# Gate and up products of 12 of 22 feature tiles as seven half products over a 2x2 block split

## The chip, the cores and the metric

The kernel runs on one core of a Trainium2 chip. The metric is device time in microseconds (us); the time before is 1137.3 us, the median of three runs (1135.86, 1137.30 and 1139.14). The engines are named as in the profile: PE is the matrix engine (PEld its loads of weights), DVE is VectorE, ACT is ScalarE, POOL is GpSimd, and SP issues the DMAs.

## The reference, cut to what matters

One layer for 512 tokens of width 1024: a SwiGLU half, a mixing stage (attention and a recurrence), and a second SwiGLU half. The change lies in the two SwiGLU halves alone:

```
def swiglu(x, w_gate, w_up, w_down):           # w_gate, w_up: 1024 x 2816; w_down: 2816 x 1024
    return (jax.nn.silu(x @ w_gate) * (x @ w_up)) @ w_down

x = x + 0.5 * swiglu(rms_norm(x, norm_ffn1), ffn1_gate, ffn1_up, ffn1_down)
...                                             # mixing
x = x + 0.5 * swiglu(rms_norm(x, norm_ffn2), ffn2_gate, ffn2_up, ffn2_down)
```

## The kernel before

The activations lie transposed: eight tiles `X[k]` of 128 features x 512 tokens. Every fp32 product is done as three matmuls of the reduced type fp32r, in `mm3` (L176 to L179): each operand is split into a high part, its cast to fp32r, and a low part, the remainder. The three are high x high (L177), high weights x low activations (L178) and low weights x high activations (L179). For a block of weights `load_split` (L154 to L164) does a DMA of 128x512, a cast on ACT (L162) and a subtraction on DVE (L163).

In `ffn` a SwiGLU half has 22 feature tiles of 128 features. For one tile, `dense` makes the gate product, 8 blocks of depth (k) x 3 matmuls of 512 columns into one PSUM bank, then the up product in the same way: 48 matmuls from four loaded blocks. The RMS norm's gain is in the split activations `xs`; its scale per token, `S`, is multiplied to both results on DVE (L296, L300). ACT does the Silu, POOL the product `h`, and `split` makes `h` into high and low (L189, L190). When the 22 hidden tiles are there, eight down products of 22 blocks x 3 matmuls follow, and DVE adds half of each to `X[m]`.

The order of work is set by a scheduler that lists the instructions of each engine by priority, in the program's order unless an instruction is not ready; tiles lie in pools with a fixed number of buffers (`NB`, `NM`, and `NW` = 3 for a raw, high or low weight block), and an instruction that writes a buffer waits until its last reader is done. Every engine then runs its list strictly in order. All weight DMAs are issued by SP, in order too.

## Time and profile before

| | |
|---|---|
| median of three runs | 1137.3 us |
| profiled execution, own time | 1135.56 us |
| its span, first to last instruction | 1133.8 us |
| first SwiGLU half: gate and up, then down | to 249 us, to 369 us |
| mixing stage | 369 to 763 us |
| second half: gate and up, then down | to 1010 us, to 1130 us |
| matmuls in the program | 6499 |
| loads of weights, of X | 256 KB each |

A matmul's row in the trace shows a start and a modelled end: the rows of successive matmuls overlap, and what one costs in a stream is the distance between starts. Names in the rows drop buffer numbers, so `g` is any gate result and `u` any up result; `wh` and `wl` are the high and low parts of a weight block, `xh` and `xl` those of the activations.

### The profile page before, as it was taken

The numbers are of one execution on the slowest core, as the hardware profiler recorded it, in microseconds if no ns is written. First come the engines' busy times: TensorE is split into PE (matmuls) and PEld (weight loads), VectorE is DVE, ScalarE is ACT, GpSimd is POOL, SyncE is SP. The second block draws the span as 40 slices with busy tenths as digits, with TensorE's granted clock in tenths as the row PEclk, the third lists the DMA queues.
The fourth block names the chain that finished last, engine by engine and source line by source line (L and its number), as shares of the span: only waits on it lengthen the run. The fifth ranks groups of instructions, "written<-read, shape, count | busy, mean of one in ns | idle before, by whom it ended". The sixth has DMA issues, their size and how long they took to land.

```text
span 1133.8 us, 16807 instructions
## 1 busy us (share of the span) xinstructions
PE 1105.7 (98%) x6499; PEld 870.7 (77%) x6499; DVE 567.3 (50%) x966; ACT 445.6 (39%) x782; POOL 182.6 (16%) x135
## 2 busy tenths in 40 slices
PE   8999999999999998999999998999999999999998
PEld 6888888888888766866677665777888888888887
DVE  7444443443333466487777777674434444433322
ACT  6333333333323553364644654553333333322221
POOL 1111111120001233221311312041111111110000
PEclk9999999999999999999999999998999999999999
DMA  5332333233333224311302102022333232334442
GB/s 203 100 96 93 102 93 102 93 90 102 99 93 104 90 66 112 88 47 40 75 27 53 39 23 57 11 74 93 93 101 96 94 102 93 103 90 116 115 114 68
DMA packets 67231, 97.79 MB, mean 86 GB/s; under 512 B 19280, under 2 KB 21456, under 8 KB 67152
## 3 DMA queue, kind: packets, MB, share of 16 engines
q1 hardware_dynamic: 67152, 96.73, 29.0%
q8 instruction: 51, 0.84, 0.3%
q14 instruction: 28, 0.23, 0.1%
HBM read 93.03 MB, written 3.67 MB: 85 GB/s over the span
## 4 chain that ended last, share of the span: by engine, by line
PE 87%; DVE 8%; ACT 2%; issue 1%; DMA 1%; SPq 0%; DVEq 0%; ACTq 0%
PE g L179 7%; PE g L178 7%; PE g L177 7%; PE dn L178 7%; PE dn L177 7%; PE u L179 7%; PE dn L179 7%; PE u L177 7%; PE u L178 7%; PE inv L566 2%; PE z L691 2%; PE o L717 1%; PE k L177 1%; PE k L179 1%; PE k L178 1%
## 5 line engine op out<-in xcount | busy, mean ns | idle before, releaser
L162 ACT CAST wh<-w 128x512 fp32r<-128x512 f32 (+1 forms) x315 | 192.1, 610 | 412.9 <-PE dn L178 146.6
L163 DVE TENSOR_TENSOR wl<-w,wh 128x512 fp32r<-128x512 f32 (+1 forms) x294 | 200.2, 681 | 246.4 <-ACT wh L162 245.7
L179 PE MATMUL g<-xh,wl 128*128 128x512 f32 x352 | 138.1, 392 | 1.9 <-DVE wl L163 1.9
L177 PE MATMUL u<-xh,wh 128*128 128x512 f32 x352 | 137.2, 390 | 2.6 <-ACT wh L162 2.6
L178 PE MATMUL g<-xl,wh 128*128 128x512 f32 x352 | 138.1, 392 | 0.7 <-DVE xl L193 0.7
L177 PE MATMUL g<-xh,wh 128*128 128x512 f32 x352 | 138.2, 393 | 0.1
L179 PE MATMUL u<-xh,wl 128*128 128x512 f32 x352 | 137.1, 390 | 0.0
L178 PE MATMUL u<-xl,wh 128*128 128x512 f32 x352 | 137.1, 389 | 0.0
L302 POOL TENSOR_TENSOR h<-sg,u 128x512 f32<-128x512 f32 x44 | 69.1, 1571 | 395.8 <-DVE u L300 386.2
L177 PE MATMUL dn<-hdh,wh 128*128 128x512 f32 x240 | 93.4, 389 | 0.0
L178 PE MATMUL dn<-hdl,wh 128*128 128x512 f32 x240 | 93.4, 389 | 0.0
L179 PE MATMUL dn<-hdh,wl 128*128 128x512 f32 x240 | 93.4, 389 | 0.0
L179 PEld LDWEIGHTS g<-xh,wl 128*128 128x128 f32 x352 | 66.8, 190 | 16.2 <-DVE wl L163 2.3
L177 PEld LDWEIGHTS u<-xh,wh 128*128 128x128 f32 x352 | 66.1, 188 | 17.1 <-ACT wh L162 3.3
L178 PEld LDWEIGHTS g<-xl,wh 128*128 128x128 f32 x352 | 66.6, 189 | 15.0 <-DVE xl L193 1.1
L177 PEld LDWEIGHTS g<-xh,wh 128*128 128x128 f32 x352 | 66.7, 189 | 14.7 <-ACT sq L134 0.5
L178 PEld LDWEIGHTS u<-xl,wh 128*128 128x128 f32 x352 | 66.2, 188 | 13.7
L179 PEld LDWEIGHTS u<-xh,wl 128*128 128x128 f32 x352 | 66.1, 188 | 13.6
L300 DVE TENSOR_TENSOR u<-u,S 128x512 f32<-128x512 f32 x44 | 30.4, 691 | 65.7 <-PE u L179 65.7
L163 POOL TENSOR_TENSOR wl<-w,wh 128x512 fp32r<-128x512 f32 x22 | 30.4, 1384 | 137.6 <-ACT wh L162 102.6
L177 PEld LDWEIGHTS dn<-hdh,wh 128*128 128x128 f32 x240 | 45.1, 188 | 9.4
L179 PEld LDWEIGHTS dn<-hdh,wl 128*128 128x128 f32 x240 | 45.1, 188 | 9.3
(268 smaller groups left out, 1798.6 us busy)
## 6 DMA issues: line engine op xcount, KB each, us to landing
w<-wgu SPq DMA_DIRECT2D x176, 256.0 KB, 2.6
w<-wd SPq DMA_DIRECT2D x80, 256.0 KB, 2.6
w<-wrw SPq DMA_DIRECT2D x28, 256.0 KB, 2.6
w<-wqk SPq DMA_DIRECT2D x16, 256.0 KB, 2.6
wv<-wv SPq DMA_DIRECT2D x16, 256.0 KB, 2.6
wo<-wo SPq DMA_DIRECT2D x16, 256.0 KB, 2.6
x<-xT SPq DMA_DIRECT2D x8, 256.0 KB, 5.4
w<-wd SPq DMA_DIRECT2D x16, 128.0 KB, 2.0
```

What stands on the lines that cost most here:

```text
L162: cp(hi[:, :n], raw[:, :n])
L163: pool.tensor_tensor(lo[:, :n], raw[:, :n], hi[:, :n].bitcast(F32), SUB)
L177: mms.append(nc.tensor.matmul(ps, lhsT=lh, rhs=rh, start=start, stop=False))
L178: nc.tensor.matmul(ps, lhsT=lh, rhs=rl, start=False, stop=False)
L179: nc.tensor.matmul(ps, lhsT=ll, rhs=rh, start=False, stop=stop)
L300: nc.vector.tensor_tensor(u, pu, S, MUL)
L302: nc.gpsimd.tensor_tensor(h, sg, u, MUL)
L566: nc.tensor.matmul(ps[rows[p], cc], lhsT=l_[rows[p], cc], rhs=r[rows[p], cc], start=True, stop=True)
L691: nc.tensor.matmul(pz[p][:, 0:L], lhsT=qh[rows[p], i * P:L], rhs=kh[rows[p], 0:L], start=True, stop=False)
L717: nc.tensor.matmul(po[rows[p], i * P:L], lhsT=Vt[b][:, hd * CH:(hd + 1) * CH], rhs=ats[p][:, b * P:(b + 1) * P], start=b == 0, stop=b == i)
```

## The change

In each SwiGLU half the first four tiles are as before. Of the other 18, every third (tiles 4, 7, ..., 19) stays a plain product; the other 12 go through `seven`. There the depth is cut into two halves of four blocks (k1, k2) and the tokens into two halves of 256 columns. Gate and up weights of a tile are then a 2x2 matrix of blocks (G1, G2; U1, U2), the activations another, and the two results for two token halves come from seven products of half depth and half width in place of eight: each has 4 k-blocks x 3 matmuls of 256 columns, 12 matmuls. Three use weight blocks as they are (G1, G2, U2), four use sums (s1 = U1+U2, s2 = s1+G1, s3 = G1+U1, s4 = G2+s2), each made on DVE and split again with a cast on ACT and a subtraction on DVE. The activations' parts that they meet are made once per half in `halves`: the eight tiles normalized with gain and scale (`xn`), and four differences of their blocks (`xy`, split to `xch`, `xcl`). PSUM banks `pa` and `pc` collect several products; partial sums are copied out on ACT or added on DVE, into `cu` (gate) and `h` (up), 256 columns at a time. The up result comes with the sign turned, so the other tiles turn theirs too and the down results are added with -0.5.

`step` lets a part of `halves` into the program after every four k-blocks of a plain product. Two `seven` tiles are interleaved by their yields. The sums take the eight buffers of `X`; so `X` is read again from DRAM before the down products, in the second half from a copy `xmid` that SP writes at its start. The mixing stage is not touched.

```
plain tile:  gate 8 k x 3 matmuls x 512 columns, up the same              48 matmuls
seven:       7 products x 4 k x 3 matmuls x 256 columns                   84 matmuls
```

```diff
+    NB = {"x": 16, "q": 3, "b": 4, "r": 10, "i": 10, "c": 6, "v": 4, "k": 4, "g": 8, "a": 4, "t": 2, "f": 4, "s": 2, "X": 8}
+    NPL = 4
...
-    X = [pc.tile([P, T], F32, name=f"x{k}") for k in range(KD)]
+    X = [slot("X", "x") for _ in range(KD)]
...
+    def mm3(ps, lh, ll, rh, rl, start, stop, again=False):
+        mms.append(nc.tensor.matmul(ps, lhsT=lh, rhs=rh, start=start, stop=False, skip_group_check=again))
...
+    HT = T // 2
+    XTAG = "iiiiiggg"
+    def halves(g, S, xn, B):
+        def blocks(h):
+            t_ = [quad("xn", tag="b") for _ in range(2)]
+            for i in range(2):
+                for q in range(2):
+                    k = 4 * h + 2 * i + q
+                    x = t_[i][:, q * T:(q + 1) * T]
+                    nc.vector.scalar_tensor_tensor(x, X[k], v(g, k), S, MUL, MUL)
+                    xn.append(split(x, "x", None, "xn"))
+                    yield
+            l, r = slice(0, HT), slice(HT, T)
+            for m, z in (((1, l),), ((2, l), (3, r)))[h]:
+                B[m] = [(hi[:, z], lo[:, z]) for hi, lo in xn[4 * h:4 * h + 4]]
+            return [[c3(t, T)[:, :, z] for t in t_] for z in (l, r)]
+        tags = iter("c" * 6 + "k" * 4 + "t" * 2 + "r" * 2 + "s" * 2)
+        def parts(m, f):
+            t_ = c3(quad("xy"), HT)
+            src = [t_[:, 2 * i:2 * i + 2] for i in range(2)]
+            r = []
+            for i in range(2):
+                f(src[i], i)
+                hi, lo = slot(next(tags), "xch", F32R), slot(next(tags), "xcl", F32R)
+                nc.scalar.copy(c3(hi, HT), src[i])
+                nc.vector.tensor_tensor(c3(lo, HT), src[i], c3(hi, HT).bitcast(F32), SUB)
+                r += [(hi[:, :HT], lo[:, :HT]), (hi[:, HT:], lo[:, HT:])]
+                if i == 0:
+                    yield
+            B[m] = r
+            yield
+            return src
+        b11, b12 = yield from blocks(0)
+        b21, b22 = yield from blocks(1)
+        yield from parts(5, lambda o, i: nc.vector.tensor_tensor(o, b11[i], b12[i], SUB))
+        y3 = yield from parts(7, lambda o, i: nc.vector.tensor_tensor(o, b22[i], b12[i], SUB))
+        y6 = yield from parts(6, lambda o, i: nc.vector.scalar_tensor_tensor(o, y3[i], -1.0, b11[i], MUL, SUB))
+        yield from parts(4, lambda o, i: nc.vector.scalar_tensor_tensor(o, y6[i], -1.0, b21[i], MUL, SUB))
+    def mm3s(ps, w, x, start):
+        for k in range(4):
+            ks = slice(k * P, (k + 1) * P)
+            mm3(ps[:, 0:HT], w[0][:, ks], w[1][:, ks], x[k][0], x[k][1], start and k == 0, k == 3, not start)
+    def seven(gate, up, need, put):
+        def sum_split(a_, b_, s):
+            t_ = slot("X", s)
+            nc.vector.tensor_tensor(t_, a_, b_, ADD)
+            hi, lo = slot("X", s + "h", F32R), slot("X", s + "l", F32R)
+            nc.scalar.copy(hi, t_)
+            nc.vector.tensor_tensor(lo, t_, hi.bitcast(F32), SUB)
+            return t_, (hi, lo)
+        def raw(tag, src, s):
+            t_ = slot(tag, s)
+            nc.sync.dma_start(t_, src)
+            return t_
+        k1, k2 = slice(0, T), slice(T, 2 * T)
+        lh, rh = slice(0, HT), slice(HT, T)
+        G1 = load(gate[:, k1], T, "wg")
+        U1, U2 = raw("f", up[:, k1], "wu"), raw("f", up[:, k2], "wu")
+        pa, pc_, pe = bank("acc", "pa"), bank("ma", "pc"), bank("mi", "pe")
+        cu, h = slot("a", "cu"), slot("a", "h")
+        mm3s(pa, w_split(G1), need(1), True)
+        with tc.high_priority(500):
+            nc.scalar.copy(cu[:, lh], pa[:, lh])
+        yield
+        s1, w = sum_split(U1, U2, "s1")
+        mm3s(pc_, w, need(5), True)
+        with tc.high_priority(500):
+            nc.scalar.copy(h[:, rh], pc_[:, lh])
+        yield
+        s2, w = sum_split(s1, G1, "s2")
+        mm3s(pa, w, need(6), False)
+        with tc.high_priority(500):
+            nc.scalar.copy(cu[:, rh], pa[:, lh])
+        G2 = load(gate[:, k2], T, "wg")
+        mm3s(pe, w_split(G2), need(2), True)
+        with tc.high_priority(500):
+            nc.vector.tensor_tensor(cu[:, lh], pe[:, lh], cu[:, lh], ADD)
+        yield
+        _, w = sum_split(G1, U1, "s3")
+        mm3s(pa, w, need(7), False)
+        with tc.high_priority(500):
+            nc.vector.tensor_tensor(h[:, rh], pa[:, lh], h[:, rh], ADD)
+        _, w = sum_split(G2, s2, "s4")
+        mm3s(pc_, w, need(3), False)
+        with tc.high_priority(500):
+            nc.vector.tensor_tensor(cu[:, rh], pc_[:, lh], cu[:, rh], ADD)
+        act(cu, cu, AF.Silu)
+        nc.vector.tensor_tensor(h[:, rh], h[:, rh], cu[:, rh], MUL)
+        yield
+        mm3s(pa, w_split(U2), need(4), False)
+        nc.vector.tensor_tensor(h[:, lh], pa[:, lh], cu[:, lh], MUL)
+        put(h)
...
+        xsrc = a["xT"]
         if last:
-            xs = norm_in(g)
+            xsrc = pd.tile([KD, P, T], F32, name="xmid")
+            for k in range(KD):
+                nc.sync.dma_start(xsrc[k], X[k])
+            xs = norm_in(g, XTAG)
...
+        home = ["v"] * 2 + ["r"] * 4 + ["q"] * 3 + ["b"] * 4 + ["i"] * 5 + ["g"] * 4
+        def put(h):
+            hid.append(split(h, home[len(hid)], None, "hd"))
+        made = {}
+        xn = []
+        hv = [None]
+        turn = [0]
+        def step():
+            turn[0] += 1
+            if hv[0] and turn[0] % 3:
+                next(hv[0], None)
+        def need(m):
+            while m not in made:
+                next(hv[0])
+            return made[m]
+        for f in range(NPL):
             if f == 0 and first:
                 pg, pu = first()
             else:
-                pg = dense(wgu[2 * f], xs, "g")
+                pg = dense(wgu[2 * f], xs, "g", step)
                 if f == 1 and first:
                     hold(5)
             if S is None:
                 S, _, _ = norm_scale(eng=nc.vector if first else nc.gpsimd)
             if f or not first:
-                pu = dense(wgu[2 * f + 1], xs, "u")
+                pu = dense(wgu[2 * f + 1], xs, "u", step)
                 if f == 0:
                     hold(5)
+            if f == 0:
+                hv[0] = halves(g, S, xn, made)
             t = slot("a", "t")
             nc.vector.tensor_tensor(t, pg, S, MUL)
             sg = slot("a", "sg")
             act(sg, t, AF.Silu)
             u = slot("a", "u")
-            nc.vector.tensor_tensor(u, pu, S, MUL)
+            nc.vector.scalar_tensor_tensor(u, pu, -1.0, S, MUL, MUL)
             h = slot("a", "h")
             nc.gpsimd.tensor_tensor(h, sg, u, MUL)
-            hid.append(split(h, home[f] if f < len(home) else "a", None, "hd"))
+            put(h)
+        old = iter(())
+        for f in range(NPL, NF):
+            if f % 3 == NPL % 3:
+                need(2)
+                next(old, None)
+                pg = dense(wgu[2 * f], xn, "g", step)
+                for _ in old:
+                    pass
+                pu = dense(wgu[2 * f + 1], xn, "u", step)
+                sg = slot("a", "sg")
+                act(sg, pg, AF.Silu)
+                h = slot("a", "h")
+                nc.vector.scalar_tensor_tensor(h, pu, -1.0, sg, MUL, MUL)
+                put(h)
+                old = iter(())
+                continue
+            new = seven(wgu[2 * f], wgu[2 * f + 1], need, put)
+            next(new)
+            next(old, None)
+            next(new)
+            for _ in old:
+                pass
+            next(new)
+            old = new
+        for _ in old:
+            pass
         for m in range(KD):
+            X[m] = slot("X", "x")
+            nc.sync.dma_start(X[m], xsrc[m])
             ps = dense(wd[m], hid, "dn")
             if last:
                 o = slot("a", "out")
-                nc.vector.scalar_tensor_tensor(o, ps, 0.5, X[m], MUL, ADD)
+                nc.vector.scalar_tensor_tensor(o, ps, -0.5, X[m], MUL, ADD)
                 nc.sync.dma_start(out[m], o)
             else:
-                nc.vector.scalar_tensor_tensor(X[m], ps, 0.5, X[m], MUL, ADD)
+                nc.vector.scalar_tensor_tensor(X[m], ps, -0.5, X[m], MUL, ADD)
```

The order of the instructions shows three places. On PE, in the first half: before, the end of a gate product and the start and end of the up product that follows it.

```order
L179 MATMUL g_145_693<-xh_30_206,wl_151_715 128x512
L177 MATMUL u_152_730<-xh_10_117,wh_154_733 128x512
L178 MATMUL u_152_730<-xl_11_118,wh_154_733 128x512
L179 MATMUL u_152_730<-xh_10_117,wl_155_734 128x512
...
L179 MATMUL u_152_730<-xh_30_206,wl_158_752 128x512
L177 MATMUL g_164_778<-xh_10_117,wh_166_781 128x512
```

After, around tiles 7 to 9: the first matmul of a plain up product and its last, then the first of each of the next nine products (`pa`, `pc` and `pe` are the banks; tile 8 has pa_254, tile 9 pa_273; `s1h`, `s2h`, ... are split sums).

```order
L184 MATMUL u_241_1025<-xnh_65_291,wh_243_1028 128x512
...
L186 MATMUL u_241_1025<-xnh_128_537,wl_247_1047 128x512
L184 MATMUL pa_254_1075<-xnh_65_291,wh_259_1080 128x256
...
L184 MATMUL pc_255_1076<-xch_140_573,s1h_262_1099 128x256
...
L184 MATMUL pa_254_1075<-xch_184_730,s2h_265_1118 128x256
...
L184 MATMUL pe_256_1077<-xnh_102_436,wh_268_1137 128x256
...
L184 MATMUL pa_273_1160<-xnh_65_291,wh_278_1165 128x256
...
L184 MATMUL pa_254_1075<-xch_152_621,s3h_281_1184 128x256
...
L184 MATMUL pc_255_1076<-xnh_102_436,s4h_284_1203 128x256
...
L184 MATMUL pc_274_1161<-xch_140_573,s1h_287_1224 128x256
...
L184 MATMUL pa_254_1075<-xch_213_864,wh_289_1241 128x256
```

The plain product of 24 matmuls per bank is followed by products of 12, and the two tiles' products are mixed.

On DVE before, a tile and a half of plain work: four remainders of weights per tile, two products with `S`, one remainder of the hidden (`hd`).

```order
L300 TENSOR_TENSOR u_142_686<-u_133_645,S_44_255 128x512
L163 TENSOR_TENSOR wl_155_734<-w_153_731,wh_154_733 128x512
L190 TENSOR_TENSOR hd_144_690<-h_143_688,hd_144_690 128x512
L163 TENSOR_TENSOR wl_158_752<-w_156_749,wh_157_751 128x512
L296 TENSOR_TENSOR t_159_767<-g_145_693,S_44_255 128x512
L163 TENSOR_TENSOR wl_167_782<-w_165_779,wh_166_781 128x512
L163 TENSOR_TENSOR wl_170_800<-w_168_797,wh_169_799 128x512
L300 TENSOR_TENSOR u_161_771<-u_152_730,S_44_255 128x512
```

After, from the product that ends the plain tile 7 (its up result `u_241`) on: remainders of weights, sums and their remainders, up to the first reading of `pe`.

```order
L458 SCALAR_TENSOR_TENSOR h_249_1064<-u_241_1025,sg_248_1062 128x512
L164 TENSOR_TENSOR wl_279_1166<-wg_270_1154,wh_278_1165 128x512
L197 TENSOR_TENSOR hd_250_1066<-h_249_1064,hd_250_1066 128x512
L164 TENSOR_TENSOR wl_290_1242<-wu_253_1073,wh_289_1241 128x512
L319 TENSOR_TENSOR s4l_285_1204<-s4_283_1201,s4h_284_1203 128x512
L316 TENSOR_TENSOR s1_286_1222<-wu_271_1156,wu_272_1158 128x512
L319 TENSOR_TENSOR s1l_288_1225<-s1_286_1222,s1h_287_1224 128x512
L316 TENSOR_TENSOR s2_292_1261<-s1_286_1222,wg_270_1154 128x512
L349 TENSOR_TENSOR cu_257_1078<-pe_256_1077,cu_257_1078 128x256
L164 TENSOR_TENSOR wl_297_1283<-wg_295_1280,wh_296_1282 128x512
L164 TENSOR_TENSOR wl_307_1343<-w_305_1340,wh_306_1342 128x512
L319 TENSOR_TENSOR s2l_294_1264<-s2_292_1261,s2h_293_1263 128x512
```

The products with `S` are gone, and sums (`s1`, `s2`) and their remainders (`s1l`, `s4l`) stand between the weights' remainders.

On SP at the start of the second half, before: the weight loads follow each other.

```order
L159 DMA w_1474_7053<-wgu2 128x512
L159 DMA w_1477_7071<-wgu2 128x512
L159 DMA w_1494_7129<-wgu2 128x512
L159 DMA w_1497_7147<-wgu2 128x512
L159 DMA w_1506_7177<-wgu2 128x512
```

After:

```order
L157 DMA w_1626_7862<-wgu2 128x512
L157 DMA w_1629_7880<-wgu2 128x512
L374 DMA xmid_7820<-x_608_2852 128x512
L374 DMA xmid_7820<-x_628_2958 128x512
L157 DMA w_1646_7938<-wgu2 128x512
L374 DMA xmid_7820<-x_648_3064 128x512
...
L374 DMA xmid_7820<-x_748_3594 128x512
L157 DMA w_1649_7956<-wgu2 128x512
```

The eight writes of `X` to `xmid` stand among and before the third and fourth weight loads.

## Rows read from the trace of the kernel before

**Rows 1.** Page, parts 1 and 4: engines; the chain that ended last:
```profile
PE 1105.7 (98%) x6499; PEld 870.7 (77%) x6499; DVE 567.3 (50%) x966; ACT 445.6 (39%) x782; POOL 182.6 (16%) x135
...
PE 87%; DVE 8%; ACT 2%; issue 1%; DMA 1%; SPq 0%; DVEq 0%; ACTq 0%
```

**Rows 2.** Windows: stretch, length, busy us (xinstructions) by engine, clock, DMA:
```profile
core 0: us, PE busy (x) PEld busy (x) DVE busy (x) ACT busy (x) POOL busy (x), PEclk, DMA share, GB/s
30.00:249.00 219.00, 219.00 (x968) 181.41 (x967) 91.84 (x141) 72.85 (x120) 31.48 (x20) 1.00 0.31 97
...
775.00:1010.00 235.00, 235.00 (x1044) 194.64 (x1043) 98.90 (x152) 79.52 (x130) 34.63 (x22) 1.00 0.31 96
```

**Rows 3.** Chain, gate and up of one tile: start us, us, what:
```profile
64.73 0.23 PE g L178
...
70.17 0.23 PE u L178
```

**Rows 4.** Other matmuls: timeline, and by line: ns min/median/max:
```profile
643.78 1.02 PE L202 MATMUL bn<-xr,cst 128*128 128x512 f32 x2
...
L202 PE MATMUL bn<-xr,cst x8: 590/592/697, 439.2 to 644.2; 128*128 128x512 f32 x8
...
721.02 0.29 PE L693 MATMUL z<-mkb,ninf 128*128 128x128 bf16 x2
...
L693 PE MATMUL z<-mkb,ninf x32: 219/229/230, 484.2 to 721.1; 128*128 128x128 bf16 x32
...
775.21 0.95 PE L215 MATMUL ms<-ones,sq 128*128 128x1 f32 x8
...
L215 PEld LDWEIGHTS ms<-ones,sq x24: 187/192/192, 19.1 to 775.9; 128*128 128x128 f32 x24
L215 PE MATMUL ms<-ones,sq x24: 164/250/250, 19.4 to 775.9; 128*128 128x1 f32 x24
```

**Rows 5.** Timeline: start us, us, engine, line, out<-in [idle before]:
```profile
100.16 0.39 PE L179 MATMUL g<-xh,wl 128*128 128x512 f32 x1
100.16 0.19 PEld L177 LDWEIGHTS g<-xh,wh 128*128 128x128 f32 x1
...
100.30 0.69 DVE L190 TENSOR_TENSOR hdl<-h,hdh 128x512 fp32r<-128x512 f32 x1 [1.83 <-ACT hdh L189]
...
100.92 0.69 DVE L163 TENSOR_TENSOR wl<-w,wh 128x512 fp32r<-128x512 f32 x1
...
102.20 0.39 PE L179 MATMUL g<-xh,wl 128*128 128x512 f32 x1
...
102.62 0.69 DVE L296 TENSOR_TENSOR t<-g,S 128x512 f32<-128x512 f32 x1 [1.02 <-PE g L179]
```

**Rows 6.** Groups by shape: busy us, mean ns; idle before, releaser:
```profile
L163 DVE TENSOR_TENSOR wl<-w,wh 128x512 fp32r<-128x512 f32 x79 | 54.2, 685 | 38.0 <-ACT wh L162 38.0
L162 ACT CAST wh<-w 128x512 fp32r<-128x512 f32 x79 | 49.0, 621 | 95.5 <-PE u L178 63.5 <-PE g L178 32.1
...
L134 ACT ACTIVATE sg<-t 128x512 f32<-128x512 f32 x20 | 12.7, 633 | 6.6 <-DVE t L296 6.6
...
L193 DVE SCALAR_TENSOR_TENSOR xl<-x,vec,xh 128x512 fp32r<-128x512 f32 x24 | 20.2, 840 | 2.2 <-ACT xh L134 2.2
L492 DVE TENSOR_TENSOR Aa<-A,cst 128x256 f32<-128x256 f32 x16 | 6.6, 414 | 5.0 <-PE A L489 5.0
L134 ACT ACTIVATE l<-l 128x256 f32<-128x256 f32 x16 | 6.2, 412 | 0.2
```

**Rows 7.** DMA issues: x count, KB each, median us to landing:
```profile
w<-wgu SPq DMA_DIRECT2D x176, 256.0 KB, 2.6
```

**Rows 8.** Timeline at the second half's start, and one DMA issue:
```profile
764.17 0.68 DVE L747 TENSOR_TENSOR x<-wo,x 128x512 f32<-128x512 f32 x1
...
771.95 0.62 ACT L162 CAST wh<-w 128x512 fp32r<-128x512 f32 x1 [5.80 <-PE g L178]
...
101.63 0.33 SPq L159 DMA_DIRECT2D w<-wgu  x1
```

More of the change, by code (lines that the diff above doesn't have):

```diff
@@ L95, in nm @@
         return f"{s}_{uid[0]}"
-    NB = {"x": 16, "q": 3, "b": 4, "r": 10, "i": 10, "c": 6, "v": 4, "k": 4, "g": 8, "a": 4, "t": 2, "f": 4, "s": 2}
+    NB = {"x": 16, "q": 3, "b": 4, "r": 10, "i": 10, "c": 6, "v": 4, "k": 4, "g": 8, "a": 4, "t": 2, "f": 4, "s": 2, "X": 8}
     NM = {"acc": 2, "sd": 1, "mi": 2, "ma": 3}
     NW = 3
+    NPL = 4
     def slot(tag, s="t", dt=F32, shape=None):
@@ L152, in layer, with load, w_split @@
     wct = [0]
-    def load_split(src, n, s="w", pool=None, cp=nc.scalar.copy):
-        if pool is None:
-            wct[0] += 1
-            pool = nc.gpsimd if mixing[0] and wct[0] % 2 else nc.vector
+    def load(src, n, s="w"):
         raw = pw.tile([P, T], F32, tag="raw", name=nm(s), bufs=NW)
         nc.sync.dma_start(raw[:, :n], src)
+        return raw
+    def w_split(raw, n=T, s="w", pool=nc.vector, cp=nc.scalar.copy):
         hi = pw.tile([P, T], F32R, tag="whi", name=nm(s + "h"), bufs=NW)
@@ L164, in load_split @@
         return hi, lo
+    def load_split(src, n, s="w", pool=None, cp=nc.scalar.copy):
+        if pool is None:
+            wct[0] += 1
+            pool = nc.gpsimd if mixing[0] and wct[0] % 2 else nc.vector
+        return w_split(load(src, n, s), n, s, pool, cp)
     mms = []
@@ L173, in hold @@
                 follow(ins, mms[n - KD])
-    def mm3(ps, lh, ll, rh, rl, start, stop):
-        mms.append(nc.tensor.matmul(ps, lhsT=lh, rhs=rh, start=start, stop=False))
-        nc.tensor.matmul(ps, lhsT=lh, rhs=rl, start=False, stop=False)
-        nc.tensor.matmul(ps, lhsT=ll, rhs=rh, start=False, stop=stop)
+    def mm3(ps, lh, ll, rh, rl, start, stop, again=False):
+        mms.append(nc.tensor.matmul(ps, lhsT=lh, rhs=rh, start=start, stop=False, skip_group_check=again))
+        nc.tensor.matmul(ps, lhsT=lh, rhs=rl, start=False, stop=False, skip_group_check=again)
+        nc.tensor.matmul(ps, lhsT=ll, rhs=rh, start=False, stop=stop, skip_group_check=again)
     def split(src, tag, scale=None, s="o"):
@@ L194, in split, with norm_in @@
         return hi, lo
-    def norm_in(g):
-        return [split(X[k], "x", v(g, k), "x") for k in range(KD)]
+    def norm_in(g, tags="x" * KD):
+        return [split(X[k], tags[k], v(g, k), "x") for k in range(KD)]
     def head_sum(ps, x):
@@ L234, in norm_scale, with gemm @@
         return S, rs, E
-    def gemm(ps, wsrc, xs):
+    def gemm(ps, wsrc, xs, step=lambda: None):
         n = len(xs)
@@ L244, in gemm, with dense @@
                 mm3(ps, wh[:, ks], wl[:, ks], xs[k][0], xs[k][1], k == 0, k == n - 1)
-    def dense(wsrc, xs, s):
+            step()
+    def dense(wsrc, xs, s, step=lambda: None):
         ps = bank("acc", s)
-        gemm(ps, wsrc, xs)
+        gemm(ps, wsrc, xs, step)
         return ps
+    HT = T // 2
[36 more added lines that the diff above has]
+        yield from parts(4, lambda o, i: nc.vector.scalar_tensor_tensor(o, y6[i], -1.0, b21[i], MUL, SUB))
@@ L272, in first @@
                                         cp=nc.scalar.copy if k or q else nc.vector.tensor_copy) for q in range(2)]
-                    xs.append(split(X[k], "x", v(g, k), "x"))
+                    xs.append(split(X[k], XTAG[k], v(g, k), "x"))
                     ks = slice(k % 4 * P, (k % 4 + 1) * P)
@@ L280, in ffn @@
         hid = []
-        home = ["q"] * NB["q"] + ["b"] * NB["b"] + [t_ for t_ in "ivkgr" for _ in range((NB[t_] - 2 * (t_ == "r")) // 2)]
-        for f in range(NF):
+        home = ["v"] * 2 + ["r"] * 4 + ["q"] * 3 + ["b"] * 4 + ["i"] * 5 + ["g"] * 4
[14 more added lines that the diff above has]
+        for f in range(NPL):
             if f == 0 and first:
```

## The prediction

> **What bounds the kernel now.** I read the page first: TensorE (PE) is busy 98% of the span and the chain that ended last runs 87% over it [rows 1]. An average over stages proves little, so next come the windows by stage. In the plain gate and up stretches, 30 to 249 us and 775 to 1010 us, PE is busy for the whole window at a granted clock of 1.00 (the 2.4 GHz level), while VectorE (DVE) and ScalarE (ACT) work 42% and 33% of it [rows 2]. The chain there is matmul after matmul: 24 of them, one gate or up product, from 64.73 to 70.17, 5.44 us, so 0.2267 us each [rows 3]. A feature tile is two such products, 48 matmuls, 10.88 us, and nothing on PE waits. So this stage is worth what its matmuls cost, and every other engine matters only if it comes to be late.
>
> **The price of a half product, the largest term.** The change does 12 of 22 tiles per half, 24 in all, as seven products of 4 k-steps, 3 matmuls each, over 256 columns: 84 half matmuls for 48 full ones. Columns fall by 84 x 256 / (48 x 512) = 0.875, which would be 1.36 us per tile if time went with columns. The break-even is 10.88 / 84 = 0.1295 us per half matmul.
>
> No matmul of this form with 256 columns is in the trace, so I bound it. Lower end: 256 columns at 2.4 GHz, one per cycle, are 0.107. Upper end: the 512-column matmul itself, 0.2267, as if halving saved nothing. Between them: 512 columns alone would be 0.213, so 0.013 of the 0.2267 is something else. The plain fp32 sums over L202 show no such excess: two matmuls last 1.02 us together and one row is 0.592, so they lie 0.43 apart, twice 0.213 [rows 4]. The bf16 matmuls of 128 columns do: two take 0.29 and one 0.219 to 0.229, so they start 0.06 to 0.07 apart where 128 columns are 0.053 [rows 4]. About 0.012 over at 128 columns and 0.013 over at 512: the excess goes with the matmul, not with its columns. So I take 0.107 + 0.013 = 0.120.
>
> A load of weights must also fit, since 84 loads replace 48. Its row is 0.19 long [rows 5], longer than 0.120. But a load's row is not the time for which it holds the next: eight loads of 128x128 with one-column matmuls pass in 0.95 us, the last row 0.25, so one per 0.10, though each row is 0.19 [rows 4]. It fits under 0.120, narrowly.
>
> With 0.120 a tile is 84 x 0.120 = 10.08 us, 0.80 less, 24 tiles: **-19.2 us**. The ends give -45 (0.107) and +196 (0.2267).
>
> [...]
>
> **What VectorE must do, and what hides it.** By the changed order a plain tile in the later part has 6 DVE operations of 512 columns (4 weight remainders, one product, one remainder of the hidden), and a seven-product tile 12 of 512 (3 weight remainders, 4 sums, 4 remainders of sums, one of the hidden) and 5 of 256. Two such tiles and a plain one repeat: 30 x 0.69 + 10 x 0.41 = 24.8 us [rows 6], against PE's 2 x 10.08 + 10.88 = 31.0 us. So DVE goes from 42% to 80%, the new engine to watch. ACT: 24 casts and Silus of 0.62 or 0.63 and 6 copies of some 0.41, 17 us.
>
> Average room is not enough; the order decides. I go through the repeat from the end of a plain up product (the place shown for DVE). PE then has four products (5.8 us) whose weights are split already. DVE first takes that up result, then in sequence the remainder for the next gate block, U2's, s4's, then s1 and s2, eight operations, 5 us at the 0.61 to 0.62 at which they start after each other [rows 5], before it waits for PE's fourth product. From there each remainder is written 2.4 us or more before PE needs it: tightest is the first up load of the plain tile (its buffer is freed only in the middle of the gate product), then s4 of the second tile at 2.8, s2 at 3.3. Each of the nine reads of PSUM waits some 0.19 us behind a matmul's end (102.20 + 0.23 to 102.62, [rows 5]); these lie inside the margins. So I cost the sums at **0**; with the margins gone the price is that of the second rival. The weight loads have the same bytes and land in 2.6 us [rows 7]; by the order of SP the tightest, the gate block that s2 needs, lands half a us before DVE reads it, over ten before PE does.
>
> **A new wait.** The changed program gives the plain up product the PSUM bank of its gate product, so its first matmul waits until ACT's Silu has read the gate; between them PE does one half product, 12 x 0.120 = 1.44 us. ACT sees the end some 0.19 later, as DVE does in [rows 5], and has one weight cast of 0.62 before the Silu of 0.63 [rows 6]: 1.44, then the release and a load. Queued behind is all of PE. I take 0.2 for each (0 to 0.3), 5 per half: **+2**.
>
> **The way in.** The eight normalized blocks cost DVE 8 x (0.84 + 0.69) = 12.2 us over tiles 1 to 3, which leave it 3 x (10.9 - 7 x 0.69) = 18 [rows 6]. The four differences cost 8 x 2 x 0.69 = 11 us, and tile 4 leaves 6.8; the rest falls into the first pair. +1 per half (0 to 4): **+2**.
>
> **The second half's start.** SP now issues eight stores of X (256 KB each) ahead of the fourth weight load. The last X is done at 764.17 + 0.68 = 764.9; with 8 issues at 0.33 and 2.6 to land the load is there at 770, and its cast began at 771.95 only [rows 5, 7, 8]. Stores before it in the queue can delay it: **+1** (0 to 5). The eight reloads of X in the down stage are queued many us before their use, with DMA at 0.31 [rows 2]: 0. The GpSimd product that goes was waited for by nothing on PE: 0. The mixing stage keeps its PE order: 0.
>
> Sum: -19.2 + 2 + 2 + 1 = -14.2. The profiled execution took 1135.56 us (span 1133.8); 1121.4 results. The median of the runs shown is 1.7 above it: **1123 us**.
>
> **Rivals.**
> *The excess shrinks with the columns.* For it: 0.0133 is just 1/16 of 0.2133, and the bf16 pair is another form than fp32r. Then a half matmul costs 0.1133, a tile 9.52, -32.6 + 5 = -27.6: 1110 us. [...]
>
> *VectorE paces the pairs.* If the margins are consumed, two seven-product tiles cost what DVE needs: 24 x 0.69 + 10 x 0.41 = 20.7 and eight waits of 0.19 = 1.5, 22.2 us against PE's 20.2. That is 2.0 for each of 12 pairs, +24: 1147 us, slower. It decides from 14.2 / 24 = 0.6 us of waiting per tile. For it: only eight X buffers for twelve sum tiles, so DVE cannot work ahead more than two or three sums. Against it: the margins above are four operations, and the plain tile lets DVE catch up by 6 us.
>
> *Weight loads do not hide behind short matmuls.* Each half matmul would cost a load row, 0.188, a tile 15.8: +118 + 5, 1260 us. For it: the row's length. Against it: the one-column chain of [rows 4]. [...]
>
> *It does not do what it says:* half matmuls land at the break-even of 0.1295, or the small waits eat the 14 us: 1137 us.
>
> **How the numbers follow.** Forecast 0.55, with its own range 1113 to 1132 (0.116 to 0.124 per half matmul, waits 3 to 9). Shrinking excess 0.20. DVE pacing 0.17. Loads 0.04, no change 0.04. The runs of before spread by 0.3%, about what a measurement can tell from no change: 1134 to 1141 is "the same". Below it lie the first two but for 0.02 of the forecast, and 0.02 of DVE's: 0.75. Within: 0.02, the no-change case and 0.04 of DVE's with small waits: 0.10. Above: 0.11 of DVE's and the loads: 0.15. For 8 in 10 I leave out half of the loads' and pacing's upper part and the lowest of the shrinking case: 1102 to 1145.
>
> **What would show it.** The spacing of 128x256 matmuls on pa, pc and pe: 0.120 confirms the main term, 0.113 the first rival, 0.19 the third. PE's idle time before the up product, put down to Silu on ACT, about 0.2 each, ten times. No PE idle time before products on s1 to s4; any put down to their remainders is the second rival. DVE near 80% in the stretch. PE waits for weights near 770 would show the stores. Wrong is the prediction if the spacing is 0.13 or more, or if PE waits over 0.6 us per tile.

## The result and the profile after

The changed kernel took 1126.95 us (median of four runs, 1125.75 to 1128.58); the kernel before took 1136.58 in the four runs beside it. The ratio is 0.9913, with an interval of 0.989 to 0.9937: faster, by about 10 us where 14 were forecast (1123), and inside the range.

One column of the tables below needs a word. The runs of one kernel differ mainly by the granted clock of TensorE: in 46 runs of the kernel before, those with a mean granted clock of 0.990 or less have spans of 1137.0 to 1140.5 us, those with 0.997 or more 1129.7 to 1132.2. Span times mean granted clock, worked out for each run, stays within 1124.4 to 1128.8 (median 1126.3). By it the changed kernel is at 1115.2, 11.1 less. Runs of one kernel still differ by up to 2 us either way in it, so less than 1 us between two medians says little. The profiled run was one with a low clock. Windows of the profile after show two of the stretches, at a granted clock of 0.50 in part (from 7.4 to 10.8 us, where matmuls of 512 columns start 0.43 apart, and from 635.5 to 642.3); the last line is the mean over the span:

```profile
5.00:10.00 5.00, 2.95 (x8) 2.11 (x8) 3.88 (x7) 2.94 (x6) 0.00 (x0) 0.74 0.96 328
634.00:642.00 8.00, 6.72 (x84) 5.08 (x85) 4.39 (x7) 2.12 (x4) 1.86 (x2) 0.59 0.14 35
...
core 0: 1126.8 us, clock 0.989
```

Each follows a stop of PE (1.51 us for the first weight block; 1.48 for a DVE result in the mixing stage). The mixing stage, whose work is unchanged, is 3.1 us longer in this profile (397.1 against 394.0). In it the stretches below 1.00 are worth 8.5 us (1 minus clock, times length), in the profile before 3.4. In other runs below, the stage, still unchanged, lasted 393.5 with 3.4 lost (e1) and 396.1 with 6.8 (e3): its length follows the clock, by some 0.6 to 0.8 us for each us lost. So span times clock takes out somewhat more than such stretches cost. Outside this stage both profiles lost 3.4 to the clock, and there the changed kernel is 10.1 us shorter.

The page after, to be read against [rows 1]: PE still bounds the kernel, with less to do, and DVE is on the chain more often.

```profile
PE 1093.4 (97%) x7363; PEld 899.4 (80%) x7363; DVE 722.2 (64%) x1258; ACT 522.1 (46%) x958; POOL 130.1 (12%) x99
...
PE 78%; DVE 14%; ACT 3%; issue 2%; DMA 2%; POOL 1%; SPq 0%; DVEq 0%; ACTq 0%; POOLq 0%
```

A window over one repeat of the seven-product stretch, against [rows 2] (busy us of PE, PEld, DVE, ACT, POOL, then clock and DMA): DVE has gone from 42% to 75%, and PE works through.

```profile
100.00:131.50 31.50, 31.50 (x220) 29.50 (x219) 23.48 (x41) 15.94 (x30) 0.00 (x0) 1.00 0.34 104
```

The main term, in the timeline after (start us, us, engine, line, out<-in), against the 0.2267 of [rows 3]:

```profile
89.54 0.40 PE L184 MATMUL g<-xnh,wh 128*128 128x512 f32 x1
...
95.00 0.28 PE L184 MATMUL pa<-xch,wh 128*128 128x256 f32 x1
95.12 0.28 PE L185 MATMUL pa<-xcl,wh 128*128 128x256 f32 x1
95.24 0.28 PE L186 MATMUL pa<-xch,wl 128*128 128x256 f32 x1
...
95.50 0.59 ACT L135 ACTIVATE sg<-g 128x512 f32<-128x512 f32 x1
...
96.44 0.40 PE L184 MATMUL u<-xnh,wh 128*128 128x512 f32 x1
...
120.62 0.40 PE L184 MATMUL g<-xnh,wh 128*128 128x512 f32 x1
```

Half matmuls start 0.12 apart (120 ns in 1937 of 1994 cases), so a half product takes 1.44. A plain tile and two seven-product tiles repeat in 120.62 - 89.54 = 31.08 us; three plain tiles would be 32.64. That is 0.78 per seven-product tile; 0.80 was forecast. The Silu ends at 96.09, 0.35 before PE wants the bank. Between the first pair's start-up and the down stage, from 88 to 246 us, PE waits for nothing at all.

What it did not get is at the way in. Products in tiles 1 and 2 of the first half last 6.02, 6.22, 5.62 and 6.20 where before only the first was over 5.5 (6.07), and in the first pair PE stands for 3 us. Counted as what PE's starts exceed 0.2267 and 0.120 by, from tile 1 to the end of the first pair, the way in costs 4.9 us more than before in the first half and 2.9 in the second (PE's count below). From the timeline and from the waits after (engine, what, for whom: us, times, longest):

```profile
38.10 0.62 ACT L196 CAST hdh<-h 128x512 fp32r<-128x512 f32 x1 [3.00 <-POOL h L444]
...
60.40 1.68 POOL L444 TENSOR_TENSOR h<-sg,u 128x512 f32<-128x512 f32 x1 [10.44 <-DVE u L442]
60.85 1.79 DVE L319 TENSOR_TENSOR s1l<-s,s1h 128x512 fp32r<-128x512 f32 x1
...
73.60 0.39 PE L184 MATMUL pa<-xch,s2h 128*128 128x256 f32 x1 [2.97 <-ACT cu L335]
...
771.59 0.62 ACT L163 CAST wh<-w 128x512 fp32r<-128x512 f32 x1 [5.25 <-PE g L185]
```

```profile
ACT hdh L196 <- POOL h L444: 7.7, 4, 3.0
```

ACT stands at the cast of h until POOL has made the product (7.7 us in four waits), and a DVE operation beside POOL's product takes 1.79 where its like take 0.69. The last timeline row is the second half's start: the late weight cast begins at 771.59, where it was 771.95 [rows 8], so the stores ahead of that load cost nothing to be seen.

### The profile page after: what moved, and what is told of

It is laid out like the page before. It is cut to its first block, busy times and chain, and to the rows that moved or that the text cites. A ratio compares the mean times of both kernels' runs of the same rounds, so it can differ in the third digit from the quotient of the medians.

```text
span 1126.8 us, 18892 instructions
## 1 busy us (share of the span) xinstructions
PE 1093.4 (97%) x7363; PEld 899.4 (80%) x7363; DVE 722.2 (64%) x1258; ACT 522.1 (46%) x958; POOL 130.1 (12%) x99
## 4 chain that ended last, share of the span: by engine, by line
PE 78%; DVE 14%; ACT 3%; issue 2%; DMA 2%; POOL 1%; SPq 0%; DVEq 0%; ACTq 0%; POOLq 0%
PE dn L185 7%; PE dn L184 7%; PE dn L186 7%; PE pa L184 4%; PE pa L186 4%; PE pa L185 4%; PE inv L736 3%; PE g L186 2%; PE g L185 2%; PE g L184 2%; PE pc L186 2%; PE pc L185 2%; PE pc L184 2%; PE u L186 2%; PE u L185 2%
## 5 line engine op out<-in xcount | busy, mean ns | idle before, releaser
L164 DVE TENSOR_TENSOR wl<-w,wh 128x512 fp32r<-128x512 f32 x198 | 135.6, 685 | 196.0 <-ACT wh L163 194.6
L163 ACT CAST wh<-w 128x512 fp32r<-128x512 f32 (+1 forms) x219 | 132.2, 604 | 239.9 <-PE dn L185 153.6
L185 PEld LDWEIGHTS dn<-hdl,wh 128*128 128x128 f32 x240 | 45.1, 188 | 9.2
L184 PE MATMUL dn<-hd,wh 128*128 128x512 f32 x112 | 43.6, 389 | 0.0
L185 PE MATMUL dn<-hd,wh 128*128 128x512 f32 x112 | 43.6, 389 | 0.0
L186 PE MATMUL dn<-hd,wl 128*128 128x512 f32 x112 | 43.6, 389 | 0.0
L186 PE MATMUL u<-xnh,wl 128*128 128x512 f32 x96 | 37.5, 390 | 0.9 <-DVE wl L164 0.9
L184 PE MATMUL g<-xnh,wh 128*128 128x512 f32 x96 | 37.6, 391 | 0.0
L185 PE MATMUL g<-xnl,wh 128*128 128x512 f32 x96 | 37.5, 391 | 0.0
L184 PE MATMUL u<-xnh,wh 128*128 128x512 f32 x96 | 37.5, 390 | 0.0
L185 PE MATMUL u<-xnl,wh 128*128 128x512 f32 x96 | 37.5, 390 | 0.0
```

The source lines that it names most:

```text
L163: cp(hi[:, :n], raw[:, :n])
L164: pool.tensor_tensor(lo[:, :n], raw[:, :n], hi[:, :n].bitcast(F32), SUB)
L184: mms.append(nc.tensor.matmul(ps, lhsT=lh, rhs=rh, start=start, stop=False, skip_group_check=again))
L185: nc.tensor.matmul(ps, lhsT=lh, rhs=rl, start=False, stop=False, skip_group_check=again)
L186: nc.tensor.matmul(ps, lhsT=ll, rhs=rh, start=False, stop=stop, skip_group_check=again)
```

## The experiments

| kernel | median us | ratio to before, interval | span x clock |
|---|---|---|---|
| before | 1137.3 (46 runs) | | 1126.3 |
| changed | 1126.95 | 0.9913 [0.989, 0.9937] | 1115.2 |
| e1 first half only | 1133.43 | 0.9951 [0.9932, 0.9969] | 1121.5 |
| e2 second half only | 1130.22 | 0.9932 [0.9909, 0.9955] | 1119.4 |
| e3 product on VectorE | 1120.80 | 0.9843 [0.9819, 0.9868] | 1108.9 |
| e4 every step | 1129.57 | 0.9936 [0.9916, 0.9957] | 1117.7 |
| e5 no plain between | 1108.75 | 0.9771 [0.9735, 0.9806] | 1102.5 |
| e6 second product on GpSimd | 1122.01 | 0.9874 [0.985, 0.9898] | 1113.6 |
| e7 sums twice | 1120.39 | 0.987 [0.9836, 0.9904] | 1109.7 |
| e8 sizes (one run, made for the spacing alone) | 1259.87 | | 1246.8 |
| e9 GpSimd product apart | 1121.90 | 0.9854 [0.983, 0.9878] | 1109.6 |
| e10 eighteen sevens | 1142.32 | 1.0035 [1.0018, 1.0052] | 1129.2 |
| e11 nineteen sevens | 1153.55 | 1.0147 [1.0118, 1.0176] | 1134.4 |
| e12 before, product on VectorE | 1137.63 | 0.9997 [0.9982, 1.0012] | 1126.8 |

### Where the missing part sits: one half at a time

```diff
-        for f in range(NPL):
+        for f in range(NF if PLAIN else NPL):     # PLAIN: this half without seven-product tiles
...                                               # (cut) nor does a plain half make `halves`
```

> Seven-product tiles in the first SwiGLU half alone; the second half has 22 plain tiles (X reloaded and xmid stored as in the changed kernel). Theory: 12 tiles save 0.80 us each = 9.6, and the way in takes back some 5 (1.9 in tiles 1 and 2, 3.0 in the wait of 73.60 in the trace of the changed kernel): 4 to 5 us faster than before, 1132. First gate and up stage near 246 us end to end or less, second again 247 long. Rival (the loss against 19.2 is spread over all 24 tiles, or sits in the mixing stage as its 3.1 us longer span suggests): each half alone gains about the half of 9.6, and the mixing stage shows the 3 us here too.

> Seven-product tiles in the second SwiGLU half alone; the first has 22 plain tiles. Theory: 9.6 saved, 2.4 taken back by the way in (waits of 0.2 to 1.2 us between 808 and 831 in the trace of the changed kernel): 7 us faster than before, 1129.5; second gate and up stage 240 us against 247, first as before. Rival (loss spread evenly): 4.8 us faster, 1132.

The first half alone gains 4.8 in span times clock, the second alone 6.9; together 11.7, and the full change has 11.1. So the two add up, and each half loses its own part of 9.6: some 5 and some 3 us. The trace of the changed kernel puts both at the way in, as the theory had it: PE's count there is 4.9 and 2.9, and in either half PE waits for nothing behind it. In the spread-evenly rival both would have gained the same.

### The price of a half matmul

```diff
-            ps = dense(wd[m], hid, "dn")
+            W = 128 if last else 256              # down products in columns of 256, then of 128
+            for c, pz in enumerate(pss): ...      # one bank for each part
+                mm3(pz[:, 0:W], wh[:, ks], wl[:, ks], hid[k][0][:, z], hid[k][1][:, z], k == 0, k == NF - 1)
```

> The kernel before, with the down products of the first half as matmuls of 256 columns (two banks) and of the second half as matmuls of 128 columns (four banks), the weights loaded before each. What counts is the distance between starts of such matmuls. Theory of the forecast (an excess of 0.013 us on each matmul whatever its size): 0.120 at 256 and 0.0667 at 128, if a load of weights (0.10 apart in the one-column chain) does not set it; then 0.10 to 0.11 at 128. Rival (1/16 of the columns): 0.113 and 0.057. Rival (a load's row is the floor): 0.19 at both. At 0.120 the first down stage of 119.45 us is 126.7; at 0.107 in the second it is 226.

From the timeline of this kernel, first half and second half:

```profile
300.05 0.28 PE L177 MATMUL dn<-hd,wh 128*128 128x256 f32 x1
300.17 0.28 PE L178 MATMUL dn<-hd,wh 128*128 128x256 f32 x1
...
1099.78 0.27 PE L177 MATMUL dn<-hdh,wh 128*128 128x128 f32 x1
1099.89 0.28 PE L178 MATMUL dn<-hdl,wh 128*128 128x128 f32 x1
```

At 256 columns 1053 of 1055 distances are 120 ns; at 128 nearly all are 110 to 114. The distances of 226.7 ns at 512 columns and 120 at 256 differ by 106.7, so 2.40 columns pass in a nanosecond, the rate of the forecast's lower end, at a granted clock of 1.00 ([rows 2] for 512; for 256 the seven-product window of the result); the bf16 matmuls of 128 columns, 66 or 67 ns apart in 13 of 14 cases in the trace of before, lie on the same line. So the excess at 256 is the same 0.013 as at 512, and a floor of 0.11 shows, only 0.01 below the half matmul. I read it as that of the loads of weights, which lie one per 0.10 in the one-column chain of [rows 4]; no run parts it from another cause. Whether the excess of this form would stay at 0.013 below 256 columns can't be seen under that floor.

### Does VectorE pace the pairs?

On the kernel of e3 (below), the sums made twice, or the plain tiles taken out:

```diff
             nc.vector.tensor_tensor(t_, a_, b_, ADD)
+            nc.vector.tensor_tensor(t_, a_, b_, ADD)          # e7
...
-            if f % 3 == NPL % 3:
+            if f == NPL:                                      # e5; e10: if False; e11: if False, NPL = 3
```

> The same kernel (products h on VectorE) with each of the four weight sums of a seven-product tile made twice: 4 x 0.60 = 2.4 us more of VectorE per such tile, 4.8 in a repeat of two such tiles and a plain one, 31.5 us long. Theory: VectorE is 23.4 us busy of 31.5, so it fits (28.9), and the margins of 2.4 to 3.3 us before PE shrink by 0.6 to 1.8 each: 0 to 3 us slower than 1120.8. Rival (the margins are nearly used up already): each of 24 tiles waits 0.5 or more, +12 us or more, 1133.

> The kernel of the run before last (products h of the first tiles on VectorE, 1120.8) with tile 4 plain and all 17 later tiles of each half as seven products: 10 plain tiles become seven-product tiles. The rival of the prediction, VectorE paces the pairs, has its case here, since no plain tile lets VectorE catch up. By its sum a tile needs 12 x 0.69 + 5 x 0.41 and 4 waits of 0.19 = 11.1 us of VectorE against 10.08 of TensorE: every one of 34 tiles 1.0 longer and none shorter, so about 10 x (11.1 - 10.9) + 24 x 1.0 = +26 us, 1147. Theory now (VectorE's operations start 0.60 and 0.34 apart, so a tile needs 12 x 0.60 + 5 x 0.34 = 8.9 and some 0.8 of waits = 9.7, under 10.08): another 10 x 0.80 = 8 us less, less what the tighter order costs, 1112 to 1118.

One window row of e7 and one of e5 (busy us by engine: PE, PEld, DVE, ACT, POOL):

```profile
100.00:131.50 31.50, 31.50 (x219) 29.21 (x219) 29.08 (x51) 17.20 (x33) 0.00 (x0) 1.00 0.34 110
```

```profile
100.00:131.50 31.50, 31.50 (x265) 31.50 (x264) 28.36 (x54) 19.45 (x39) 0.00 (x0) 1.00 0.35 107
...
100.00:160.00 60.00, 60.00 (x503) 60.00 (x502) 54.48 (x103) 36.79 (x72) 0.00 (x0) 1.00 0.34 104
```

With twice the sums DVE is 29.08 of 31.50 us busy and PE still works through the whole window: 0.8 us over e3 by span times clock, none in the median, so no more than the runs differ by. Without plain tiles DVE is busy 28.36 of 31.50 and PE does not wait either; ten more seven-product tiles gain 6.4 by span times clock (8 expected). VectorE does not pace the pairs in this order. My sum for it was too dear: rows of 0.69 and 0.41 overlap, and the operations start 0.60 and 0.34 apart.

> Products on VectorE, four plain tiles first, then all 18 others as seven products: one more seven-product tile per half than the run without plain tiles between (1108.75; 1102.6 in span times clock). Theory: 2 x 0.80 = 1.6 us less if the differences of the activations are ready: 1107 (1101). Rival: without the plain tile 4 VectorE has not made the differences when the first pair needs them, and the first products wait 1 to 5 us per half: 1109 to 1115.

> As the last, with three plain tiles first and 19 seven-product tiles per half. Theory: the way in now lacks a tile: VectorE needs for blocks, differences and first sums some 35 operations of 0.60 = 21 us besides its usual work of 7 x 0.60 a tile, and has two tiles (22 us, 8.4 of them taken) before the first pair, so some 5 us of waits per half against 0.8 gained: 1112 to 1118. Rival (the products of the first pair that need whole blocks alone give it time): no waits, 1106.

Both lost much more than either theory said. e11's mean clock is lower as well (0.984 or 0.985 in five of six runs), and whether its own stops of PE caused that no run shows: if they did, its price is the 16 us of its median, if not, the 8 of the last column. The window of e10, the largest of ACT's waits from 100 to 220 us (total, times, longest), and the timeline of PE in the first pair:

```profile
100.00:160.00 60.00, 58.65 (x470) 57.14 (x470) 51.59 (x97) 34.73 (x67) 0.00 (x0) 1.00 0.29 91
```

```profile
ACT wh L163 <- DMA wg<-wgu: 19.3, 11, 2.3
```

```profile
65.38 0.28 PE L186 MATMUL pa<-xch,s3l 128*128 128x256 f32 x1
65.50 0.33 PE L184 MATMUL pc<-xnh,s4h 128*128 128x256 f32 x1
65.66 0.28 PE L185 MATMUL pc<-xnl,s4h 128*128 128x256 f32 x1
65.96 0.39 PE L184 MATMUL pe<-xnh,wh 128*128 128x256 f32 x1
66.18 0.28 PE L185 MATMUL pe<-xnl,wh 128*128 128x256 f32 x1
66.48 0.38 PE L184 MATMUL pa<-xch,wh 128*128 128x256 f32 x1
```

PE now leaves products after their first two matmuls, those that need the high part of the weights alone, takes up another and comes back later; starts around such a change lie 0.16 to 0.30 us apart in these rows. It does so to the end of the stage: half matmuls are 130.0 ns apart on average over the trace, though most still 120; e5's average is 120.0. Yet DVE is less busy (51.59 of 60 against 54.48), and so are ACT and the DMA, so it is no engine's capacity. PE's list itself has this broken order, set by the scheduler. That the plain tile 4 keeps the products whole is shown by e5 against e10, which differ in nothing else. Why the list breaks, and why it does not recover after the first pair, stays open. One more difference is on record: e10's ACT waits 19.3 us in eleven waits for gate blocks to land, e5's for none; whether that is a cause of the order or comes from it was not tested.

### The way in

```diff
-            if hv[0] and turn[0] % 3:
+            if hv[0]:                                   # e4
```

> The changed kernel with a part of the activations' blocks and differences let in after every four k-blocks of tiles 1 to 4, not after two of three, so that all are in the program before the first pair. Theory: the wait of 3.0 us at the first pair comes from ScalarE's queue, where the copy of pa stands behind the cast of s4, whose sum is late on VectorE behind the last differences; with these earlier it goes: 3 us in the first half, 0.5 to 1 in the second, less 0 to 2 for fuller tiles 1 to 3: 1 to 4 us faster than the changed kernel. Rival (the amount of VectorE work in tiles 1 to 6 decides, wherever it stands): the wait only moves into tiles 1 to 4, and the time is the same within 1 us.

Slower by 2.5 (span times clock), and the wait at the first pair is still 2.7 us: theory and rival both fell. From the waits of e4, those of the first pair on PE and those of DVE from 24 to 67 us:

```profile
PE pa L184 <- ACT cu L335: 2.7, 1, 2.7
...
DVE hdl L197 <- ACT hdh L196: 5.5, 3, 1.8
```

The cast of s4 now stood behind the copy in ACT's queue, so its place was not the cause. But DVE stood 5.5 us behind casts of h, which waited for POOL; in the changed kernel it was 1.8 in the same stretch.

```diff
-            nc.gpsimd.tensor_tensor(h, sg, u, MUL)
+            nc.vector.tensor_tensor(h, sg, u, MUL)      # e3: first four tiles of each half
```

> The changed kernel with the products h of the first four tiles on VectorE instead of GpSimd. Theory: in tiles 1 to 3 the casts of h stand in ScalarE's queue until GpSimd's product of 1.3 us is there (1.4 to 3.0 us), weight casts queue behind them, and a VectorE operation beside the product takes 1.78 instead of 0.68; both go, so the four products of tiles 1 and 2 return from 6.02, 6.22, 5.62, 6.20 to nearly 5.44 and the second half's from 6.66: 1.5 to 3 us faster than the changed kernel, 1124 to 1125.5. The wait of 3.0 at the first pair stays. Rival (the way in is simply too much VectorE work): VectorE gets 0.69 more per tile, and it is the same or up to 2 us slower.

Faster by 6.3 in span times clock, twice what the theory gave, and the wait at the first pair, which it said would stay, is gone: all products of both pairs last 1.44. DVE's windows of 44 us from the start of tile 1's gate product, in the changed kernel, in e3 and in e9 (busy us, operations):

```profile
21.77:65.77 44.00, 39.35 (x61) 1.00 0.38 114
```

```profile
20.42:64.42 44.00, 41.21 (x70) 1.00 0.38 118
```

```profile
20.36:64.36 44.00, 41.35 (x67) 1.00 0.38 117
```

In the same time e3's DVE gets 70 operations done, three of them the products, and the changed kernel's 61. It came to the first pair six operations behind, 3.6 us at 0.60 each, and there PE stood 3.0. Two things held it, and its trace has both: the product beside it on POOL (three rows of 1.78 or 1.79, each 1.1 over its like) and the queue of ACT that waits for the product (the 1.8 us behind the cast of h). e4 has one such row there and the longer stops, and is slower, which speaks for the queue. Two runs were made to part them.

```diff
+            nc.gpsimd.tensor_tensor(slot("s", "dummy"), sg, u, MUL)                       # e6, beside e3's product
...                                                                                        # (cut) `one` is 128x1
+            a_ = nc.gpsimd.tensor_scalar(one, u[:, 0:1], 1.0, None, MUL)                  # e9, instead
+            follow(nc.gpsimd.tensor_tensor(slot("s", "dummy"), cst[:, 0:T], cst[:, 0:T], MUL), a_)
```

> The same kernel (products h on VectorE), and GpSimd makes each of these products a second time into a tile that nobody reads. It keeps GpSimd's load on the memory beside VectorE (a VectorE operation of 1.78 instead of 0.68), but nothing waits for GpSimd and the engines' lists are those of the faster kernel. Theory A (the hold of VectorE beside GpSimd made the way in slow): most of the loss comes back, 3 to 6 us slower, 1124 to 1127. Theory B (ScalarE's queue standing at the cast of h until GpSimd's product is there, and the order of the list that follows from it, made it slow): within 1 us of 1120.8, though VectorE rows of 1.78 are there.

e6 lost 4.7 in span times clock (1.2 in the median; its runs had higher clocks), but at least 2.6 of it not by the cause meant (PE's waits of 1.5 and 1.1 at the two first pairs): POOL's second product took 11.24 us, and DVE's product of tile 4 waited for a buffer that it held, in the second half a remainder in its place. Timeline of e6:

```profile
58.83 11.24 POOL L445 TENSOR_TENSOR dummy<-sg,u 128x512 f32<-128x512 f32 x1 [5.51 <-ACT s1h L318]
...
70.10 0.69 DVE L459 SCALAR_TENSOR_TENSOR h<-u,sg 128x512 f32<-128x512 f32 x1 [1.19 <-POOL dummy L445]
```

> As the run with the second product on GpSimd, but so that no buffer hangs on it: GpSimd takes one column of u into a tile of its own and then multiplies a constant tile with itself into a tile that nobody reads, at the time when the changed kernel makes its product there. The engines' lists are otherwise those of the kernel with products on VectorE (1120.8). In the run before, at the first pair VectorE waited 1.19 us for a buffer that the second product held, so its 4.7 us (span times granted clock: 1113.6 against 1108.9) mixed two causes. Theory A (VectorE held beside GpSimd): rows of 1.78 on VectorE, and 1.5 to 4 us slower than 1108.9 in span times clock. Theory B (waits in ScalarE's queue for GpSimd's result, and the lists that follow from them): within 0.7 us of 1108.9.

e9 costs 0.7 us in span times clock, at the edge of what theory B allows, and 1.1 in the median; its runs lie from 1108.6 to 1111.2, e3's from 1107.6 to 1109.2. DVE is three operations behind e3 (the third window above). But a buffer was in the way here too: the second product lies in `s`, whose two buffers also take the last parts of the activations. In the second half DVE stood 1.10 us for it, and behind that PE stood 1.04. By PE's count e9 loses 2.4 us more than e3 at the way in, 1.3 of it behind this buffer. Timeline of e9:

```profile
819.65 0.69 DVE L290 TENSOR_TENSOR xcl<-xy,xch 128x512 fp32r<-128x512 f32 x1 [1.10 <-POOL dummy L448]
...
823.64 0.39 PE L184 MATMUL pa<-xch,s2h 128*128 128x256 f32 x1 [1.04 <-ACT cu L335]
```

And e9's long rows on DVE are shorter, 1.10 to 1.53, some 4.6 us in all over their like where the changed kernel has 6.5. So what is shown is that POOL's product at the way in costs the 6.3 us, and that holds on DVE of e9's size cost about 1 us by each of these measures. That the other 5 come from ACT's queue standing for POOL's result, and from the changed list, is what is left by difference; no run has that wait without the hold, and both add to the same lateness of DVE, so the shares in the changed kernel stay open.

> The kernel before with its products h of all tiles on VectorE instead of GpSimd. Asks whether the 6 us that this edit gave the changed kernel were to be had before. Theory: no; VectorE was 42% busy there and TensorE waited for nothing in those stages: 1137 within 1 us. Rival: the hold beside GpSimd cost the kernel before as well: 3 to 6 us faster, 1132.

The same edit in the kernel before, there for all tiles, gives nothing: ratio 0.9997. There, too, ACT waits for four products between 24 and 67 us (the waits of before):

```profile
ACT hd L189 <- POOL h L302: 7.0, 4, 2.1
```

But DVE has half its time free there [rows 2]. It is the change that made POOL's product cost.

## Why the prediction was right, and where its terms were not

The time came out between the forecast and no change because the largest term was right and one small one was not. *The price of a half product*, -19.2: right to 0.02 per tile, and for the reason given. The excess of 0.013 stays with the matmul; loads fit, with 0.01 to spare if the floor of 0.11 is theirs. *VectorE's cover at 0*: right; 75% busy (23.48 of 31.50) where I had said 80%, and e7 shows room for 2.4 us more per tile. *The new wait for the Silu*: mis-sized, 0.2 each forecast, none there. ACT is done 0.35 us ahead. What is left is 5.47 against 5.44 per plain product, in gate products too, which wait for no Silu (the first five starts behind a half product lie 2 to 9 ns further apart); that is some 0.06 per plain tile, +0.6 and not +2. I had put a weight cast and the Silu in a row behind the gate's end; the cast began before it. *The second half's start*: +1 forecast, none seen. *The mixing stage at 0*: right, its 3.1 us were the clock.

*The way in*, +1 per half, is the step that failed: 4.8 and 2.7 us (9.6 less the gains of e1 and e2, the plain tiles' 0.3 each among them). I had compared DVE's free time with its work, and these do nearly fit, as e3 shows (0.9 us lost in the first half, none in the second, by PE's count). What I left out was that the first four tiles keep POOL's product, beside which three of DVE's operations took 1.78 or 1.79 in place of 0.69, and for whose result ACT's queue stood 7.7 us in four waits; I had said of the product that goes that nothing on PE waited for it, and took that for the one that stays. With DVE half free this cost nothing that could be seen (e12: 1126.8 against 1126.3 in span times clock); with DVE full to the brim lost time came back as a late weight; which of the two weighs more there is not settled. With the measured terms the sum is -19.2 + 4.8 + 2.7 = -11.7 (the 0.6 of the plain tiles lies in these), and span times clock gives -11.1. That the forecast missed by only 3 to 4 us is in part luck: the Silu and the stores, 2.4 too high, made up for part of the way in, some 5 too low.

Of the rivals, a shrinking excess and loads that do not hide are out by the spacing. VectorE as the pace-maker is out for this order, but the loss in e10 shows how near a broken order lies: 0.010 us per half matmul there eat the whole gain of the seven products.

## What to carry to other kernels

Price a smaller matmul as its columns plus the excess that the large one shows (0.013 us here, at 512 and at 256 columns), and check for a floor beneath (0.11 here, at 128). When a change fills an engine that was half idle, look for every slow helper beside it, and every queue in which the helper's result is awaited in order: in this case such holds and waits cost nothing to be seen before (e12) and 6.3 us after (e3). Here the helper's product moved to the full engine let that engine get more done (70 operations against 61), and e5, with it and without plain tiles between, is the best version: 1108.75 us, 2.3% under the kernel before.

## What the hardware showed unexpectedly

In e9 GpSimd's operation on a single column took 0.66 us in tile 0 and 10.21 in tile 3, while VectorE made 18 operations without a gap; the timelines of POOL and of DVE, and the window of DVE:

```profile
27.48 0.66 POOL L446 TENSOR_SCALAR one<-u 128x1 f32<-128x1 f32 x1 [5.28 <-DVE u L442]
...
57.62 10.21 POOL L446 TENSOR_SCALAR one<-u 128x1 f32<-128x1 f32 x1 [5.45 <-DVE u L442]
...
67.69 0.68 DVE L462 SCALAR_TENSOR_TENSOR h<-u,sg 128x512 f32<-128x512 f32 x1
...
57.62:67.83 10.21, 10.21 (x18) 1.00 0.38 121
```

The trace does not show why. Two such rows were long: the one of 10.21 ends 0.14 us after VectorE takes up the product at 67.69, the first operation since the row's start that has one input in PSUM (`u`), and one of 4.79 from 46.38 ends 0.15 us after the next such operation began, at 51.02. Two were short: the one of 0.66 and one of 1.18 from 33.85 end 0.18 and 0.14 us after the start of operations that read SBUF alone (at 27.96 and 34.89). So no rule follows from these four. In the changed kernel VectorE's row of 1.79 us, from 60.85, ends 0.56 us after POOL's product beside it; what held it there is not shown either.

A stop of TensorE of 1.5 us was followed by 3.4 us at a granted clock of 0.50 in one run (after) and by 1.00 in another (before). Timeline and window at the start of the kernel before, and the same stop after, where the window had 0.74:

```profile
7.45 0.50 PE L177 MATMUL u<-xh,wh 128*128 128x512 f32 x1 [1.55 <-ACT wh L162]
...
5.00:10.00 5.00, 3.45 (x15) 2.37 (x14) 4.16 (x7) 3.20 (x6) 0.00 (x0) 1.00 0.93 327
```

```profile
6.66 0.47 PE L184 MATMUL g<-xh,wh 128*128 128x512 f32 x1 [1.51 <-DVE wh L163]
```

Such stretches are what span times granted clock takes out of the comparison, most of the 1% by which runs of one kernel differ: spans of before lie from 1129.7 to 1140.5 us, the product from 1124.4 to 1128.8.
